# A norm listed earlier, a projection spread further and one more key buffer in a two-layer hybrid decoder

## The chip, the cores and the metric

One core of one Trainium2 chip runs the whole kernel in one launch. The metric is the device time of the core in microseconds, the median of several runs.

## The reference

Two decoder layers over 1024 positions of width 1024, all in float32. Cut to what matters:

```python
for layer in range(2):
    h = rms_norm(x, norm_mix[layer])
    q_a, k_a, v_a, q_h, f_h, i_h, g_h = split(h @ w_in[layer])
    attn = dilated_attention_group(q_a, k_a, v_a)       # 8 heads of 64; windows (128,1), (512,4), (2048,16)
    attn = rms_norm(attn, attn_out_gain[layer])         # over all 512 columns of the 8 heads
    rec = hgrn2_group(q_h, f_h, i_h, g_h)               # 4 heads of 128, gated linear recurrence
    x = x + concat([attn, rec]) @ w_out[layer]
    h = rms_norm(x, norm_mlp[layer])
    x = x + square(relu(h @ w_up[layer])) @ w_down[layer]
return rms_norm(x, norm_final)
```

The attention of each head is done over three dilated windows, whose results are merged by their softmax denominators. The attention norm needs all eight heads of a position, so it can't start on a half of the sequence before the last head has finished that half.

## The kernel before

All activations are kept transposed, as tiles of 128 columns by 512 positions, and the sequence has two halves of 512. Every float32 product is done as three products of a high and a low part (`split`, L321: ScalarE writes the high part, VectorE the low part). Such a tile is one "slot" of 2 KB per partition, and there are 71 slots that all stages share. Tiles that belong to a fixed kind have pools of their own; `COUNT` (L38) holds how many buffers each pool has.

**The order of the work.** The kernel first lists all its operations in a program order, and `Program.order` (L137) then makes the order of each engine's instructions from it. It is a list planner: whenever an engine is free in its model, it takes the operation with the lowest number in the list among those whose inputs are ready and whose buffers are free. An operation may be taken ahead of the list, as long as it is not more than 60 us of TensorE work beyond the oldest operation not yet started (36 us for loads and stores, which SyncE issues; `LOOKAHEAD`, L40). It may not take a buffer that the operations before it in the list will need. On the chip each engine then runs its instructions in that fixed order, so an instruction that waits holds up all that stand behind it on its engine. SyncE's queue issues all loads and stores.

`weave` (L46) sets the program order between two streams: it always advances the one with the smallest count of steps over weight. `weave((a, 24), (b, 13))` thus takes 24 steps of `a` to 13 of `b`, and when one stream is empty, the rest of the other follows.

**The stage around the change.** In each layer the steps come as follows.
- Two HGRN stages (the recurrence woven with the projections), the second with the attention's first projection.
- Attention heads 0 to 3, six units each, woven with the attention's second projection (L1198).
- Attention heads 4 to 7, six units each, woven with `out_part(1)` (L1200). That is the output projection of the HGRN half: for each half of the sequence one step that loads 8 tiles of HGRN results, then 8 steps of one block each. A block (`gemm4`) is 12 matmuls of 512 columns, a load of the residual tile and an addition.
- `norm_attn(0)` and `norm_attn(1)`, the attention norm of each half (L1189): squares, a sum over partitions by matmul, logarithm and exponential, then four scaled tiles, each split in two.
- `out_part(0, xs, (0,))`, the output projection of the attention half for positions 0 to 511, then for the second half, woven with the norm ahead of the MLP.

An attention unit (`attention`, L1128) is one head's 256 queries against their keys. Units 0 and 1 of a head serve the first half, 2 and 3 the second, 4 and 5 are the strided far window, which goes to the second half alone. A unit does the scores (L941, two matmuls for each block of 128 queries: high and low part of the keys), the maximum and mask on VectorE with a statistic (`ls`), the exponential on ScalarE, transposes, and the products with the values. After unit 1 of head 7 the last row of the first half is divided (`divide`, L991); after unit 5 the second half's is merged (`merge`, L998). Both send statistics through DRAM: a transpose on TensorE (`lt`), a copy (`lrow`), a store, a load, in `merge` small steps of VectorE and ScalarE (`ml`, `mw`) and another store, and a load that spreads the result over partitions (`rb`).

**The keys.** `Head.k` (L903) loads a head's high and low keys into two buffers of pool `kk`, 4 KB per partition each, by two DMAs each. Before, the pool has three. The MLP's up projection uses the same pool (`norm_up`, L1208): `hilo(..., "b11", p < COUNT["kk"])` puts an operand pair in a `kk` buffer for as many of its four pairs as there are buffers, and in two slots otherwise.

Of the kernel before, what the change touches and what calls it, by code (L numbers as in the profile page):

```python
# [34 lines left out]
EARLY = 10  # L35


COUNT = {"kk": 3, "slot": 71, "raw": 4, "trig": 2, "whi": 8, "wlo": 8, "ls": 4, "last": 2, "row": 2, "rc": 4, "z": 2, "gemm": 3, "sc": 2, "tr": 2, "acc": 1,  # L38
         "dram": 1 << 20, "const": 1 << 20}
LOOKAHEAD = {"PE": 60e3, "SP": 36e3}  # L40
PATIENCE = 5e3
# [4 lines left out]
def weave(*parts):  # L46

    live = [[0, *p] if isinstance(p, tuple) else [0, p, 1] for p in parts]
    while live:
        part = min(live, key=lambda p: p[0] / p[2])  # L50
        part[0] += 1
        if next(part[1], live) is live:
            live.remove(part)
# [69 lines left out]
class Program:  # L123
# [13 lines left out]
    def order(self):  # L137
        free = dict(COUNT)
        busy = {e: 0.0 for e in self.LATENCY}
# [30 lines left out]
        while done < len(self.ops):  # L170
            while oldest < len(self.ops) and self.ops[oldest].start is not None:
                oldest += 1
            for e in ready:
# [3 lines left out]
                while ready[e]:  # L177
# [12 lines left out]
                    for t, at in need.items():  # L190
                        h = held[t][oldest:max(at)]
                        ok = ok and free[t] >= len(at) and (not len(h) or h.max() + len(at) <= COUNT[t])
                    if not ok:
# [61 lines left out]
def trunk(ctx: ExitStack, tc: tile.TileContext, xT, wts, cols, trig, toep, lmask, ident_d, out):  # L255
# [7 lines left out]
    dram = ctx.enter_context(tc.tile_pool(name="dram", bufs=1, space=bass.MemoryType.DRAM))  # L263
    pools = {t: sbuf for t in COUNT}
    pools.update({t: psum for t in ("gemm", "sc", "tr", "acc")}, dram=dram, const=const)
# [25 lines left out]
    def slot(name, dt=F32, shape=None, width=None):  # L291
        return Buf(name, "slot", shape or [128, W], dt, width)

    def bank(name, tag, width=None):
        return Buf(name, tag, [128, W], F32, width)
# [13 lines left out]
    def tt(dst, a, b, kind, n=W, extra=()):  # L309

        op("DVE", c_tt(n), [dst[0]], [x[0] for x in (a, b) if x[0] is not None] + list(extra),
           lambda e: V.tensor_tensor(dst[1](), a[1](), b[1](), op=kind))  # L312

    def whole(b):
        return b, lambda: b.t
# [27 lines left out]
    def load(dst, view, src, nbytes, src_buf=None, join=False):  # L343
        op("SP", max(650.0, nbytes / 360.0), [dst], [src_buf] if src_buf else [], lambda e: nc.sync.dma_start(view(), src()), join=join)
# [46 lines left out]
    def gemm4(ps, grps, m, hf, acts, ts=slice(0, W)):  # L391
        gemm(ps, [grps[m // 4].piece(m % 4)], [x[hf] for x in acts], ts)
# [118 lines left out]
    def table():  # L511
        return [[None] * NH for _ in range(KT)]
# [4 lines left out]
    def load_x(src, k, hf):  # L517
        x = slot(f"x{k}_{hf}")
        i, j = rows(k, hf)
        saved = src and src[k][hf]  # L520
        if saved:
            load(x, lambda: x.t, lambda: saved.t, 1 << 18, saved)
        else:
            load(x, lambda: x.t, lambda: xT[i, j], 1 << 18)
        return x
# [16 lines left out]
    xs, hs, rs, xsaved = table(), table(), {}, None  # L542
# [34 lines left out]
    for l in range(L):  # L577
# [363 lines left out]
        def scores(hd, n, st, at):  # L941

            sp, t, ps = [], None, None
            k2 = [hd.k(part) for part in range(2)]
            for i, (q, q0, keys, x0) in enumerate(blocks(hd, n)):
                w = len(range(*keys.indices(S)))
                if t is None or o + w > W:
                    t, ps, o = slot("sp"), bank("sc", "sc"), 0

                def emit(e, ps=ps, q=q, q0=q0, keys=keys, o=o, w=w):  # L950
                    for part, k in enumerate(k2):
                        PE.matmul(ps[:, o:o + w], lhsT=q[:, q0:q0 + 128], rhs=k[:, keys], start=part == 0, stop=part == 1)  # L952

                op("PE", 2 * c_mm(w), [ps], [q] + k2, emit, join=o > 0)

                def emit(e, ps=ps, t=t, o=o, w=w, m=st.part(at + i), x0=x0):
                    V.tensor_tensor_reduce(t[:, o:o + w], ps[:, o:o + w], tpt[:, x0:x0 + w], -0.125, 3e38,  # L957
                                           OP.add, OP.min, m.t)

                op("DVE", c_tt(w), [t, st.part(at + i)], [ps, tpt], emit, join=True)  # L960
                sp.append((t, o, w))
                o += w
            return sp

        def soft(sp, st, at):
            for i, (t, o, w) in enumerate(sp):
                m, sum_ = st.part(at + i), st.part(at + 8 + i)
                op("ACT", c_act(w) + 190, [t, sum_], [t, m], lambda e, t=t, o=o, w=w, m=m, sum_=sum_: A.activation(  # L968
                    t[:, o:o + w], t[:, o:o + w], AF.Exp, bias=m.t, scale=-1.0, accum_out=sum_.t), "ln", True)
# [21 lines left out]
        def divide(st, ar):  # L991

            cs = slice(8, 16)
            op("DVE", 110.0, st.all(cs), st.all(cs), lambda e: V.reciprocal(st.buf[:, cs], st.buf[:, cs]))
            rb = spread(rows_of(st, cs), 0, "rb")
            tt(whole(ar), whole(ar), whole(rb), OP.mult)
# [131 lines left out]
        def attention(units):  # L1128
            for h, n in units:
                key = h  # L1130
                if key not in heads:
                    heads[key] = Head(h)
                hd, p, hf = heads[key], h // 2, int(n > 1)
                if (p, hf) not in stats:
                    stats[p, hf] = Stats()
                    left[p, hf] = 8 if hf else 4
                    araw[p][hf] = slot(f"ar{p}_{hf}")
                if n > 3 and p not in far_:
                    far_[p] = [slot("ar4") for _ in range(2 if p in SIDE else 1)]
                st = stats[p, hf]  # L1140
                at = 16 * (n > 3) + h % 2 * 4 + n % 2 * 2
                sp = scores(hd, n, st, at)
                soft(sp, st, at)
                if n > 3 and p in SIDE:
                    strided(h, n, sp, far_[p][n % 2])
                else:
                    values(h, n, sp, far_[p][0] if n > 3 else araw[p][hf])
                left[p, hf] -= 1
                if not left[p, hf]:
                    if hf:  # L1150
                        merge(st, araw[p][1], far_[p])
                    else:
                        divide(st, araw[p][0])
                yield
# [3 lines left out]
        def out_part(part, xs, hfs=(0, 1)):  # L1158
            acts, grp = mixed[4 * part:4 * part + 4], grp_out[part]
            for hf in hfs:  # L1160
                if part:
                    for h in range(HH):
                        pair = []
                        for d in hout[h][hf]:
                            y = slot("mh", F32R)
                            load(y, lambda y=y: y.t.bitcast(F32), lambda d=d: d.t, 1 << 18, d)
                            pair.append(y)
                        mixed[4 + h][hf] = pair
                    acts = mixed[4:]
                    yield  # L1170
                for m in range(KT):
                    if part:
                        xs[m][hf] = load_x(xsaved, m, hf)
                    ps = bank("pso", "gemm")
                    gemm4(ps, grp, m, hf, acts)
                    tt(whole(xs[m][hf]), whole(xs[m][hf]), whole(ps), OP.add)
                    yield
# [8 lines left out]
        def units(hs_, ns):  # L1186
            return [(h, n) for h in hs_ for n in ns]

        def norm_attn(hf):  # L1189
            r = rstd([araw[k][hf] for k in range(4)], 512, "an", hf == 0)  # L1190
            yield
            for k in range(4):
                t = slot("ant")
                stt(whole(t), whole(araw[k][hf]), lambda c=C_ATT + l * 4 + k: col(c), whole(r))
                mixed[k][hf] = hilo(t, f"ma{k}_{hf}")
                yield

        weave((attention(units(range(0, 4), range(6))), 26), (attn_proj(1), 12))  # L1198
        xs = table()
        weave((attention(units(range(4, 8), range(6))), 24), (out_part(1, xs), 13))  # L1200
        weave(norm_attn(0))
        weave(norm_attn(1))
        weave(out_part(0, xs, (0,)))

# [3 lines left out]
        def norm_up(hf):  # L1208
# [8 lines left out]
            for p in range(4):  # L1217
# [3 lines left out]
                if hf == 0:  # L1221
                    bo["11"].append(hilo(hf32[p][0], "b11", p < COUNT["kk"]))
                    bo["21"].append(hilo(hf32[p + 4][0], "b21"))
# [144 lines left out]
        xs = table()  # L1368
# [93 lines left out]
        last = l + 1 == L  # L1462
# [16 lines left out]
    for o in prog.order():  # L1479
        for b in o.fresh:  # L1480
            single = b.tag in ("dram", "const")
            b.tile = pools[b.tag].tile(b.shape, b.dt, name=b.name, tag=b.name if single else b.tag,
                                       bufs=1 if single else COUNT[b.tag])
        if o.on == "ACT" and o.table and o.table != loaded:
# [91 lines left out]
```

## Time and profile before

| | |
|---|---|
| median of 3 runs | 2428.82 us (2427.02 to 2429.88) |
| the profiled execution | 2435.95 us |
| its span, first to last instruction | 2434.2 us |
| TensorE busy | 2390.8 us (98%) |
| VectorE busy | 1733.8 us (71%) |
| ScalarE busy | 1217.5 us (50%) |
| DMA queue of SyncE | 404.93 MB, 49.7% of 16 engines' span |
| mean granted TensorE clock | 0.993 |

How to read it: PE is TensorE, DVE is VectorE, ACT is ScalarE, SPq is SyncE's queue. A row names an instruction by its line, what it writes and what it reads (`sc<-k,hd`: scores from keys and a head's queries). A bracket behind a row is the idle time before it and what ended it. The granted clock is a share of the full 2.4 GHz. In the first layer the two attention stages run from about 345 to 585 us, in the second from about 1550 to 1790.

### The profile page before, as it was taken

The page shows a single profiled execution, that of the slowest core. Times are in us where ns is not written, and L with a number is a line of the kernel's source. Part 1 is how long each engine was busy: PE and PEld are TensorE (multiplying, and loading weights), DVE is VectorE, ACT ScalarE, POOL GpSimd, SP SyncE. Part 2 cuts the span into 40 slices and gives each one's busy share as a digit, 9 for nine tenths or more (in the row PEclk, how much of TensorE's full clock was granted, in tenths as well). Part 3 has the DMA queues.
Part 4 walks back from the last instruction along what each step waited for, and adds up shares of the span by engine and source line. Part 5 has one row for each costly group of instructions (what it writes and reads, how often), then busy time and mean ns, then how long its engine had stood idle before and what let it go on. Part 6 is the DMA issues. An engine that isn't in the chain of part 4 may idle for free.

```text
span 2434.2 us, 35321 instructions
## 1 busy us (share of the span) xinstructions
PE 2390.8 (98%) x12572; PEld 2029.5 (83%) x12572; DVE 1733.8 (71%) x3414; ACT 1217.5 (50%) x2391; POOL 0.2 (0%) x4
## 2 busy tenths in 40 slices
PE   9999999999999999999999999999999999999998
PEld 7888898887888878888888988898878888888887
DVE  6365877778988667765744668677889885786575
ACT  7233346665744554445532433466656455554453
POOL 0000000000000000000000000000000000000000
PEclk9999999999999999999999999999999999999999
DMA  4011365953455469656420114668344653786562
GB/s 177 27 35 53 130 212 174 272 159 122 160 207 195 152 216 317 222 181 226 169 83 18 62 53 150 209 177 267 120 165 147 225 181 138 261 310 224 182 218 94
DMA packets 189681, 407.19 MB, mean 167 GB/s; under 512 B 22656, under 2 KB 25536, under 8 KB 189504
## 3 DMA queue, kind: packets, MB, share of 16 engines
q1 hardware_dynamic: 189504, 404.93, 49.7%
q8 instruction: 99, 1.62, 0.3%
q14 instruction: 78, 0.64, 0.1%
HBM read 291.37 MB, written 113.48 MB: 166 GB/s over the span
## 4 chain that ended last, share of the span: by engine, by line
PE 91%; DMA 4%; DVE 2%; ACT 2%; SPq 0%; issue 0%; DVEq 0%; ACTq 0%
PE psd L1415 8%; PE psd L1416 8%; PE psd L1417 8%; PE psu L1264 8%; PE psu L1265 8%; PE psu L1266 8%; PE sc L952 2%; PE pa L705 2%; PE pso L383 2%; PE pso L382 2%; PE pso L384 2%; PE pv L1115 1%; PE psv L407 1%; PE psq L382 1%; PE psv L408 1%; PE psv L409 1%
## 5 line engine op out<-in xcount | busy, mean ns | idle before, releaser
L325 DVE TENSOR_TENSOR al<-al,ah 128x512 fp32r<-128x512 f32 x224 | 152.7, 686 | 51.3 <-ACT ah L323 50.7
L323 ACT CAST ah<-al 128x512 fp32r<-128x512 f32 x224 | 137.4, 618 | 97.9 <-DMA al<-a 50.9
L968 ACT ACTIVATE sp<-sp,ls 128x256 f32<-128x256 f32 (+2 forms) x192 | 100.0, 523 | 17.7 <-DVE ls L957 17.3
L957 DVE CUSTOM_DVE_ANT_0 sp<-sc,tpt 128x256 f32<-128x256 f32 (+1 forms) x192 | 83.1, 439 | 35.6 <-PE sc L952 34.0
L952 PE MATMUL sc<-k,hd 128*128 128x256 f32 (+3 forms) x384 | 95.0, 358 | 12.7 <-DMA k<-kl 7.2
L952 PEld LDWEIGHTS sc<-k,hd 128*128 128x128 f32 x384 | 61.2, 195 | 19.6 <-DVE ls L957 6.1
L1247 ACT ACTIVATE c<-c 128x512 f32<-128x512 f32 x96 | 60.5, 630 | 33.2 <-DVE c L312 33.0
L323 ACT CAST pth<-ptr 128x512 fp32r<-128x512 f32 (+1 forms) x96 | 51.3, 552 | 39.5 <-PE ptr L1102 38.1
L1248 ACT ACTIVATE c<-c 128x512 f32<-128x512 f32 x108 | 68.4, 633 | 3.4
L325 DVE TENSOR_TENSOR ptl<-ptr,pth 128x512 fp32r<-128x512 f32 (+1 forms) x96 | 60.7, 641 | 10.9 <-ACT pth L323 9.8
L705 PEld LDWEIGHTS pa<-q,k 128*112 128x112 f32 (+3 forms) x512 | 62.0, 184 | 3.4
L705 PE MATMUL pa<-q,k 128*112 128x64 f32 (+3 forms) x512 | 61.2, 262 | 0.0
L312 DVE TENSOR_TENSOR x<-x,psd 128x512 f32<-128x512 f32 (+1 forms) x68 | 41.8, 652 | 25.3 <-PE psd L1417 25.1
L312 DVE TENSOR_TENSOR x<-x,pso 128x512 f32<-128x512 f32 x64 | 43.4, 681 | 15.2 <-PE pso L384 14.7
L1102 PE MATMUL ptr<-ident,sp 128*128 128x128 f32 x352 | 53.3, 276 | 0.5 <-ACT sp L968 0.4
L1264 PE MATMUL psu<-bt3h,s3h 128*128 128x512 f32 x128 | 50.6, 395 | 3.2 <-ACT u L319 3.2
L1122 ACT COPY pvt<-pv 64x256 f32<-64x256 f32 x80 | 29.6, 370 | 47.0 <-PE pv L1115 45.5
L713 DVE COPY_PREDICATED at<-lmt,pa 126x256 f32<-126x256 uint8 (+1 forms) x64 | 32.8, 512 | 25.1 <-PE pa L705 24.4
L1265 PE MATMUL psu<-bt3l,s3h 128*128 128x512 f32 x128 | 50.3, 393 | 0.0
L1266 PE MATMUL psu<-bt3h,s3l 128*128 128x512 f32 x128 | 50.3, 393 | 0.0
L1265 PE MATMUL psu<-bt1l,s1h 128*128 128x512 f32 x128 | 49.8, 389 | 0.0
L1266 PE MATMUL psu<-b22h,s4l 128*128 128x512 f32 x128 | 49.8, 389 | 0.0
(4980 smaller groups left out, 8136.0 us busy)
## 6 DMA issues: line engine op xcount, KB each, us to landing
al<-a SPq DMA_DIRECT2D x96, 256.0 KB
w0u<-in_wts_dram SPq DMA_DIRECT2D x42, 512.0 KB
w1u<-in_wts_dram SPq DMA_DIRECT2D x42, 512.0 KB
a<-c SPq DMA_DIRECT2D x76, 256.0 KB
al<-a0t SPq DMA_DIRECT2D x64, 256.0 KB
al<-a1t SPq DMA_DIRECT2D x64, 256.0 KB
hd<-q SPq DMA_DIRECT2D x48, 256.0 KB
a0t<-t SPq DMA_DIRECT2D x48, 256.0 KB
```

The costliest lines, as they stand in the source:

```text
L312: lambda e: V.tensor_tensor(dst[1](), a[1](), b[1](), op=kind))
L323: op("ACT", c_act(n), [hi[0]], [src[0]], lambda e: A.copy(hi[1](), src[1]()), join=join)
L325: lambda e: V.tensor_tensor(lo[1](), src[1](), hi[1]().bitcast(F32), op=OP.subtract), join=join)
L705: PE.matmul(pa[0:128 - b, c * 64:c * 64 + 64], lhsT=k[:, c * 128:c * 128 + 128 - b], rhs=by_half(q)[:, c, :, 1, :], start=True, stop=True)
L952: PE.matmul(ps[:, o:o + w], lhsT=q[:, q0:q0 + 128], rhs=k[:, keys], start=part == 0, stop=part == 1)
L968: op("ACT", c_act(w) + 190, [t, sum_], [t, m], lambda e, t=t, o=o, w=w, m=m, sum_=sum_: A.activation(t[:, o:o + w], t[:, o:o + w], AF.Exp, ...
L1264: PE.matmul(ps.t, lhsT=wh[:, cs], rhs=xh.t, start=first and k == 0, stop=False, skip_group_check=True)
L1265: PE.matmul(ps.t, lhsT=wh[:, cs], rhs=xl.t, start=False, stop=False, skip_group_check=True)
L1266: PE.matmul(ps.t, lhsT=wl[:, cs], rhs=xh.t, start=False, stop=k == 3, skip_group_check=True)
L1415: PE.matmul(ps.t, lhsT=wh[:, cs], rhs=th.t[:, ts], start=first and j == 0, stop=False, skip_group_check=True)
L1416: PE.matmul(ps.t, lhsT=wh[:, cs], rhs=tl.t[:, ts], start=False, stop=False, skip_group_check=True)
L1417: PE.matmul(ps.t, lhsT=wl[:, cs], rhs=th.t[:, ts], start=False, stop=j == 15, skip_group_check=True)
```

## The change

There are three edits. The key pool gets a fourth buffer, and the slots go from 71 to 69, which is the same memory. By the expression in `norm_up` all four pairs then lie in key buffers. The first half's norm is put into the attention's stream of steps between unit 2 and unit 3 of head 7; it has five steps, so the stream has 29. The weights of that weave go from 24 : 13 to 34 : 13.

```diff
-COUNT = {"kk": 3, "slot": 71, "raw": 4, "trig": 2, "whi": 8, "wlo": 8, "ls": 4, "last": 2, "row": 2, "rc": 4, "z": 2, "gemm": 3, "sc": 2, "tr": 2, "acc": 1,
+COUNT = {"kk": 4, "slot": 69, "raw": 4, "trig": 2, "whi": 8, "wlo": 8, "ls": 4, "last": 2, "row": 2, "rc": 4, "z": 2, "gemm": 3, "sc": 2, "tr": 2, "acc": 1,
...
         weave((attention(units(range(0, 4), range(6))), 26), (attn_proj(1), 12))
         xs = table()
-        weave((attention(units(range(4, 8), range(6))), 24), (out_part(1, xs), 13))
-        weave(norm_attn(0))
+        last = itertools.chain(attention(units(range(4, 7), range(6)) + units((7,), range(3))), norm_attn(0),
+                               attention(units((7,), range(3, 6))))
+        weave((last, 34), (out_part(1, xs), 13))
         weave(norm_attn(1))
         weave(out_part(0, xs, (0,)))
```

## Rows read from the trace of the kernel before

**Rows 1.** the page, part 1: busy us, share, instructions
```profile
PE 2390.8 (98%) x12572; PEld 2029.5 (83%) x12572; DVE 1733.8 (71%) x3414; ACT 1217.5 (50%) x2391; POOL 0.2 (0%) x4
```

**Rows 2.** windows: us, busy by engine (count), clock, DMA share, GB/s
```profile
340.00:585.00 245.00, 231.90 (x1376) 201.77 (x1375) 190.35 (x477) 150.36 (x397) 0.00 (x0) 0.99 0.61 183
585.00:890.00 305.00, 305.00 (x1340) 251.35 (x1340) 239.93 (x384) 172.91 (x295) 0.00 (x0) 1.00 0.51 178
1545.00:1790.00 245.00, 233.21 (x1367) 202.67 (x1366) 189.49 (x476) 149.26 (x396) 0.00 (x0) 0.97 0.59 182
```

**Rows 3.** TensorE's waits, first layer's attention: total, times, longest
```profile
PE sc L952 <- DMA k<-kl: 4.0, 4, 1.9
...
PE pso L382 <- ACT ma_0h L323: 1.5, 1, 1.5
...
PE pso L383 <- DVE ma_0l L325: 0.7, 1, 0.7
```

**Rows 4.** the same view, second layer's attention
```profile
PE sc L952 <- DMA k<-kl: 3.2, 3, 2.2
PE sc L952 <- DVE ls L957: 3.0, 2, 2.5
...
PE pso L383 <- DVE ma_0l L325: 0.4, 1, 0.4
```

**Rows 5.** windows of 5 us behind gaps, both layers
```profile
495.00:500.00 5.00, 3.11 (x15) 2.56 (x13) 2.53 (x7) 2.05 (x4) 0.00 (x0) 0.84 1.05 276
500.00:505.00 5.00, 5.00 (x31) 4.69 (x30) 2.41 (x8) 2.59 (x10) 0.00 (x0) 0.82 0.76 216
555.00:560.00 5.00, 4.19 (x11) 2.88 (x11) 4.77 (x10) 1.94 (x4) 0.00 (x0) 0.66 0.00 0
1580.00:1585.00 5.00, 5.00 (x21) 4.12 (x20) 2.82 (x11) 2.92 (x10) 0.00 (x0) 0.66 1.03 265
1755.00:1760.00 5.00, 2.08 (x11) 1.34 (x10) 4.89 (x10) 3.55 (x7) 0.00 (x0) 0.79 0.04 8
1760.00:1765.00 5.00, 5.00 (x13) 3.79 (x14) 4.41 (x10) 1.65 (x3) 0.00 (x0) 0.53 0.00 0
```

**Rows 6.** timeline, SyncE's queue, first layer: start, us, instruction
```profile
354.85 0.35 SPq L344 DMA_DIRECT2D hd<-q  x1
368.16 1.12 SPq L344 DMA_DIRECT2D k<-kl  x2
```

**Rows 7.** windows of heads 4 to 7, line L382's instructions alone
```profile
452.00:474.50 22.50, 4.98 (x12) 2.27 (x12) 1.00 0.87 237
474.50:495.00 20.50, 5.66 (x14) 2.67 (x14) 1.00 0.93 292
495.00:521.00 26.00, 6.50 (x16) 3.06 (x16) 0.93 0.53 146
521.00:553.00 32.00, 8.91 (x22) 4.18 (x22) 1.00 0.39 125
```

**Rows 8.** timeline of VectorE, end of the first layer's attention
```profile
544.18 0.69 DVE L312 TENSOR_TENSOR ar<-ar,rb 128x512 f32<-128x512 f32 x1
...
553.13 0.74 DVE L455 SCALAR_TENSOR_TENSOR ant<-ar,colt,anrs 128x512 f32<-128x512 f32 x1
...
558.91 0.37 DVE L312 TENSOR_TENSOR mw<-ml 8x128 f32<-8x128 f32 x1
```

**Rows 9.** timeline of TensorE, the same place and behind it
```profile
550.19 0.27 PE L975 MATMUL lt<-ident,ls 128*32 128x128 f32 x1
...
554.58 0.49 PE L382 MATMUL pso<-ma_0h,w0o000h 128*128 128x512 f32 x1 [1.53 <-ACT ma_0h L323]
...
568.45 0.39 PE L382 MATMUL pso<-ma_0h,w0o010h 128*128 128x512 f32 x1
...
580.23 0.39 PE L382 MATMUL pso<-ma_1h,w0o000h 128*128 128x512 f32 x1
```

## The prediction

> **What bounds the kernel now.** First the busy shares: TensorE is busy for 2390.8 of 2434.2 us [rows 1], so every gain has to come from its 43 us of idle time, from stretches in which its clock is halved, or from other work getting out of its way. Then the stretches by stage: the attention of each layer (340 to 585 and 1545 to 1790) holds 13.1 and 11.8 us of that idle time, while the 305 us after the first has none [rows 2]. The change touches just this stage in both layers. Then what TensorE waited for there. In the first layer the score matmuls stand 4.0 us for keys that a DMA brings, and the output projection 1.5 and 0.7 us for the two parts of the normed attention output [rows 3]. In the second layer these are 3.2 us for keys and 0.4 us for the low part of the normed output, and 3.0 us behind the statistics that VectorE reads out with the scores [rows 4]; the row for the high part is the same there, word for word.
>
> Last the clock. It falls to its lower level of 1.2 GHz behind some of these gaps. In a 5 us window with a mean clock of 0.84 the lost time is 5 x 0.16 = 0.8 us. Behind the key gap at 497 the windows show 0.84 and 0.82, together 1.7 us; behind the key gap of 2.2 us at 1578 they show 0.66, 1.7 us; behind the first half's norm they show 0.66 at 555 (1.7 us) and 0.79 with 0.53 at 1755 (3.4 us) [rows 5]. The same pair of gaps cost twice as much in the second layer as in the first.
>
> Run against profile: the profiled execution took 2435.95 us, the median of the runs is 2428.82, 7.1 us (0.3%) less. The terms below are microseconds out of the profile and are taken off the median unscaled.
>
> **The change part by part.**
>
> *Fourth key buffer (T1).* A head needs two key buffers, its high and its low part. With three, the next head's low part can be loaded only when the last score matmul of the current head has let one go. SyncE takes its list in order: after the query load at 354.85 nothing is issued until the low keys go out at 368.16, 13 us in which every later load and store stands behind that one instruction [rows 6]. With four, both parts of the next head have free buffers as soon as the head before the current one is done, a head (20 to 32 us, [rows 7]) ahead. No instruction is added and no byte more moves. At most this takes away 4.0 + 3.2 = 7.2 us of gaps [rows 3, 4] and 1.7 + 1.7 = 3.4 us of slow clock [rows 5], 10.6 us. At least it gives nothing, if another load comes late in the keys' place: the DMA engines are 0.87 and 0.93 busy in heads 4 and 5 [rows 7]. But the keys of heads 1 to 3 are loaded before that, and with them go 2.1 of the first layer's 4.0 us (all but the longest, 1.9, which is head 6's) and the second layer's 2.2 us wait, so I stay near the upper end: **-8 us**.
>
> *First half's norm listed before the last three units (T2).* The norm's instructions (squares and their sum, two sum matmuls, logarithm and exponential, four scaled tiles and their split) are the same in number and hold no DMA; only their rank in the planner's list changes. In the trace the first half's row is divided at 544.18, the first scaled tile comes at 553.13 [rows 8], and the projection starts on it at 554.58 after its 1.53 us wait [rows 9]. Had the tiles been there, TensorE would have lost neither 1.5 + 0.7 + 1.7 us in the first layer nor 1.5 + 0.4 + 3.4 in the second (the 0.4 is its wait for the low part) [rows 3 to 5], 9.2 us together. But the second half's work sets a later end: from the transpose of the last statistics at 550.19 to the first product with the second half's tile at 580.23 are 30.0 us, a chain of DMAs to DRAM and back, small VectorE steps and another norm [rows 9]. The only work under it is the first half's projection: four blocks of it run from 568.45 to 580.23 [rows 9], less about 0.9 us for the sum matmuls in between, so 2.7 us a block and 22 us for its eight. If that starts earlier and the chain doesn't, the time comes back as a wait at the head of the second half. The chain can start earlier, since VectorE does the norm's eight tile operations right before the merge's first step at 558.91, with 5.4 us of norm work between 553.13 and there (5.8 us less one 0.4 us addition) [rows 8]. Bounds 0 and -9.2; I take half, **-4.6 us**.
>
> *What the norm displaces (T3).* Ranked higher, its 5.4 us of VectorE work per layer stands ahead of the last three units' score and value steps, in order. TensorE has blocks of the projection to run meanwhile, so I count **0**. If that cover is gone, the merge chain starts up to 5.4 us later in each layer, +10.8 us. The gain on the other side, a chain that starts earlier, is in T2.
>
> *HGRN projection spread (T4).* Before, the 18 steps of this projection go 13 to 24 attention steps; now 13 to 34, over 29 steps with the norm's five. When the last unit is listed, 11 rather than 13 steps are, so 7 rather than 5 are left behind it: 2 blocks, 5.4 us more work that can lie under the merge chain. Against that, the loads are listed later, and SyncE looks only 36 us of TensorE work ahead. Four products of the first weight form make a block, so heads 4 to 7 used 3, 3.5, 4 and 5.5 blocks as filler [rows 7], more than any list order demands: the filler is taken whenever attention has to wait. In head 6 (six units, 34 / 13 = 2.6 to a step) the new list lets loads go out for about 6 / 2.6 = 2.3 steps, of which one loads the second half's HGRN tiles: 1.3 new blocks and what is left over, against 4 used. If 1.6 blocks lack there, 1.6 x 2.7 = 4.4 us a layer stand idle; if attention runs through faster for it, nothing; if the lighter load traffic ends the second layer's wait for the statistics, 3.0 us are won [rows 4]. I take the end nearer to the filler rows but small, **+2 us** for both layers, since the work not done there lies under the chain later.
>
> *Two general buffers fewer (T5).* In the up projection nothing changes: its fourth pair of operands moves from two general buffers into the fourth key buffer, so 71 - 2 and 69 leave the same 69. Elsewhere 3% fewer buffers mean less prefetch. Where TensorE has no gap [rows 2] the cover holds; in attention the loads may come later. Between 0 and 7.2 us (as much as the keys cost, [rows 3, 4]); **+1.5 us**.
>
> Sum: -8 - 4.6 + 0 + 2 + 1.5 = -9.1 us; 2428.8 - 9.1 = 2419.7, forecast **2420 us**.
>
> Two rules are weighed beside this. On the clock: the Trainium skill (TensorE: Matmul & The Clock Gate, "What's actually happening") says that the slow clock is the default which activity lifts, and that the monitor behind it runs free of the kernel's start. By it a gap need not cost its drop, nor does a drop go for certain with its gap; the sum without clock terms would have T1 at 7.2 and T2 at 4.1 at most. The unequal price of the same two gaps [rows 5] agrees. On transfers: the Trainium skill (DMA: Bandwidth & Descriptors, "Specifications") gives some 358 GB/s of HBM to a core. By that the 237 and 292 GB/s of heads 4 and 5 [rows 7] leave room to load keys earlier and all of T1 could come; by their busy shares there is hardly any.
>
> **The rivals.**
> - *Everything goes.* Key gaps, norm gaps and their drops all vanish, because the spread leaves enough filler for the chain: -10.6 - 9.2 = -19.8, **2409 us**. For it: 5.4 us of extra filler against the 30 - 22 = 8 us that the chain now outlasts its projection blocks. Against it: DMA shares near full [rows 7].
> - *The norm's gain is handed back.* The chain doesn't move, T2 is zero, and of the keys only the waits outside heads 5 and 6 go: 4.0 - 1.9 (the longest, at head 6) = 2.1, and 3.2, and one drop of 1.7, 7.0; less T4 and T5, -3.5: **2425 us**. For it: the chain's DMAs are untouched. Against it: 5.4 us of VectorE work leaves the chain's start.
> - *Slower: the merge chain starts late.* The norm ahead of the last units holds VectorE for 5.4 us, so the last scores, the statistics' transpose and all behind it slip; TensorE runs out of filler and its clock falls, 5.4 + 1.7 a layer, 14.2 in all, less 8 for the keys: +6.2, **2435 us**. It decides from the point at which filler left behind the last unit is under 30 + 5.4 us; 22 of first-half projection plus two to five blocks of 2.7 is 27 to 36, so it is close. Against it: the divided row is ready only at 544.18 [rows 8], when the last scores are nearly done.
> - *The change doesn't do what it says.* The general buffers run short, the query and value loads keep SyncE as late as before, and the keys come no sooner: no change, **2429 us**. For it: 3% fewer buffers in a stage that fills them; against it: the low keys are freed by their own pool alone.
>
> **How the numbers follow.** Chances: forecast 0.42 (own range 2413 to 2424), everything 0.18, handed back 0.21, slower 0.15, nothing done 0.04. A measurement of this kernel can tell about 0.2%, 4.9 us, from no change. Faster by more than that (under 2424): the first two and a little of the third, 0.63. Within it: 0.22, the rest of the third and the fifth. Slower: 0.15. The range for 8 in 10 reaches from below the second case to between the third and the fourth: 2406 to 2433.
>
> **What would show it.** T1: no wait of the score matmuls for keys in the list of waits, both key loads issued about a head ahead, no 13 us hole in SyncE's list. T2: the norm's scaled tiles done before the last value products, no wait at the first projection product, and the time from the statistics' transpose to the second half's first product under 30 us, or covered. T3 and T4: the transpose no later against the end of head 6, and HGRN blocks still running under the chain. T5: no new waits for queries, values or weights, and TensorE still without gaps outside attention. The forecast is wrong if the idle time of the two attention stages (25 us now) falls by less than 4 us, if it reappears as waits of the second half's projection, or if other stages grow.

## The result, and the profile after

The changed kernel takes 2414.03 us (2408.34 to 2417.86, 7 runs) against 2427.02 us before (2420.86 to 2429.88, 7 runs, the three of the table above among them). The ratio is 0.9938, with a 95% interval of 0.9927 to 0.9949: 15.0 us of 2427 (12.4 to 17.7). The two medians lie 13.0 us apart, which the interval holds; below, all times go by the ratios. The forecast was 2420 us, with 2406 to 2433 as its range.

The two profiled executions lie further apart: 2435.95 and 2411.42 us. The one of before is 8.9 us above its median of seven, the one of after 2.6 below, so by the medians 11.5 of the 24.5 us between them belong to these two executions and not to the change. The views below show where time went; its amount is taken from the runs.

Page and stages of the changed kernel (windows: us, busy of TensorE, its loads, VectorE, ScalarE, GpSimd, clock, DMA share, GB/s):

```profile
span 2409.6 us, 35371 instructions
...
PE 2380.3 (99%) x12572; PEld 2025.0 (84%) x12572; DVE 1730.1 (72%) x3414; ACT 1215.3 (50%) x2391; POOL 0.2 (0%) x4
```

```profile
340.00:585.00 245.00, 239.51 (x1413) 209.91 (x1413) 197.39 (x491) 157.46 (x409) 0.00 (x0) 0.99 0.63 195
585.00:890.00 305.00, 305.00 (x1341) 251.28 (x1340) 240.46 (x386) 172.86 (x297) 0.00 (x0) 1.00 0.52 179
1545.00:1790.00 245.00, 238.82 (x1413) 208.84 (x1412) 199.48 (x491) 158.72 (x411) 0.00 (x0) 0.99 0.60 188
```

The idle time of TensorE went from 13.1 and 11.8 us in the two attention stages to 5.5 and 6.2, and the stage behind is as full as it was [rows 2]. What TensorE still waits for in the whole kernel (total, times, longest):

```profile
PE ptr L1102 <- ACT sp L968: 3.1, 6, 0.7
PE pv L1115 <- DVE ar L1124: 2.2, 5, 0.6
PE sc L952 <- DVE ls L957: 2.2, 2, 1.1
...
PE pv L1115 <- DVE ptl L325: 1.6, 3, 1.0
...
PE pso L382 <- ACT w1o110h L323: 1.4, 1, 1.4
...
PE sc L952 <- DMA hd<-q: 1.0, 2, 0.8
```

No score matmul waits for keys, and no projection matmul for a normed tile, in either layer [rows 3, 4]. What is left in the two attention stages stands behind exponentials, the rows that value products add to, low parts of transposed exponentials, statistics, queries and, once in the second layer, a weight cast.

SyncE's queue at the place of [rows 6] (start, us, instruction):

```profile
343.32 1.09 SPq L344 DMA_DIRECT2D k<-kh  x2
344.45 1.24 SPq L344 DMA_DIRECT2D k<-kl  x2
...
354.51 0.58 SPq L344 DMA_DIRECT2D hd<-q  x1
367.09 0.48 SPq L344 DMA_DIRECT2D k<-kh  x1
```

Both parts of the keys of head 1 go out at 343 and 344; before, the low part left at 368.16. But the queue still stands from 354.51 to 367.09, now for the keys of head 2: the fourth buffer has moved what waits there one head on, and not ended the hole.

The clock at its two drops in these stages, and a window at the place where the first half's norm cost one before [rows 5]:

```profile
465.00:470.00 5.00, 4.19 (x16) 3.89 (x17) 2.71 (x9) 2.01 (x6) 0.00 (x0) 0.58 0.54 186
470.00:475.00 5.00, 5.00 (x22) 3.97 (x21) 4.42 (x10) 3.70 (x10) 0.00 (x0) 0.74 1.00 268
...
545.00:550.00 5.00, 5.00 (x24) 4.13 (x23) 4.48 (x11) 3.14 (x7) 0.00 (x0) 1.00 0.01 2
...
1670.00:1675.00 5.00, 3.65 (x17) 2.83 (x16) 2.61 (x9) 2.10 (x7) 0.00 (x0) 0.91 0.93 329
1675.00:1680.00 5.00, 5.00 (x27) 4.36 (x26) 4.04 (x13) 4.22 (x14) 0.00 (x0) 0.74 0.82 193
```

The lost time is 5 x (0.42 + 0.26) = 3.4 us in the first layer and 5 x (0.09 + 0.26) = 1.8 us in the second; before it was 3.4 and 6.8 (the 6.8 with a pair of windows at 1660 that [rows 5] leave out). At 545 the clock is full.

The end of the first layer's attention on VectorE, then on TensorE:

```profile
527.31 0.69 DVE L312 TENSOR_TENSOR ar<-ar,rb 128x512 f32<-128x512 f32 x1 [1.55 <-DMA rb<-l]
...
535.20 2.08 DVE L455 SCALAR_TENSOR_TENSOR ant<-ar,colt,anrs 128x512 f32<-128x512 f32 x3 [1.36 <-ACT anrs L319]
...
544.38 0.37 DVE L312 TENSOR_TENSOR mw<-ml 8x128 f32<-8x128 f32 x1
```

```profile
534.91 0.27 PE L975 MATMUL lt<-ident,ls 128*32 128x128 f32 x1
534.94 0.48 PE L382 MATMUL pso<-mh,w0o103h 128*128 128x512 f32 x1
...
547.27 0.39 PE L382 MATMUL pso<-mh,w0o113h 128*128 128x512 f32 x1
...
547.95 0.39 PE L382 MATMUL pso<-ma_0h,w0o000h 128*128 128x512 f32 x1
...
569.39 0.40 PE L382 MATMUL pso<-ma_1h,w0o000h 128*128 128x512 f32 x1
```

The cast of the second half's first normed tile on ScalarE, before and then after:

```profile
578.48 1.94 ACT L323 CAST ma_1h<-ant 128x512 fp32r<-128x512 f32 x3 [0.82 <-DVE ant L455]
```

```profile
563.42 1.95 ACT L323 CAST ma_1h<-ant 128x512 fp32r<-128x512 f32 x3 [0.82 <-DVE ant L455]
```

The last row of the first half is divided at 527.31, the first scaled tile starts at 535.20, 9.2 us ahead of the merge's first step at 544.38, and it is used only at 547.95, behind the last HGRN block. From the transpose of the last statistics at 534.91 to the second half's first product at 569.39 are 34.5 us [rows 9: 30.0]. They are filled by four HGRN blocks, seven and a half of the eight of the first half and the last value products, with two gaps of 0.3 us before 542. The chain itself is as long as it was: the first tile's cast starts 28.3 us behind the transpose before and 28.5 after. What grew is the work under it; the tile is used 6.0 us after its cast starts, before it was 1.8. The HGRN blocks in the stretches of heads 4 to 7, the last up to 541, can be counted from line L382, four instructions to a block:

```profile
447.00:465.00 18.00, 3.31 (x8) 1.55 (x8) 1.00 0.83 233
465.00:495.00 30.00, 6.84 (x16) 3.31 (x16) 0.89 0.90 265
495.00:514.00 19.00, 3.96 (x10) 1.92 (x10) 1.00 0.63 207
514.00:541.00 27.00, 8.90 (x22) 4.17 (x22) 1.00 0.25 77
```

That is 2, 4, 2.5 and 5.5 blocks, and the other 2 behind 541, against 3, 3.5, 4 and 5.5 with none left [rows 7].

### The profile page after: what moved, and what is told of

It reads as the page before. It is cut to its first block, busy times and chain, and to the rows that moved or that the text cites. A ratio compares the mean times of both kernels' runs of the same rounds, so it can differ in the third digit from the quotient of the medians.

```text
span 2409.6 us, 35371 instructions
## 1 busy us (share of the span) xinstructions
PE 2380.3 (99%) x12572; PEld 2025.0 (84%) x12572; DVE 1730.1 (72%) x3414; ACT 1215.3 (50%) x2391; POOL 0.2 (0%) x4
## 4 chain that ended last, share of the span: by engine, by line
PE 93%; DMA 2%; DVE 2%; ACT 1%; SPq 0%; issue 0%; DVEq 0%
PE psd L1416 8%; PE psd L1418 8%; PE psd L1417 8%; PE psu L1265 8%; PE psu L1266 8%; PE psu L1267 8%; PE sc L952 2%; PE pa L705 2%; PE pso L382 2%; PE pso L384 2%; PE pso L383 2%; PE pv L1115 2%; PE psva L407 1%; PE psv L407 1%; PE psb L382 1%; PE psq L382 1%
## 5 line engine op out<-in xcount | busy, mean ns | idle before, releaser
L968 ACT ACTIVATE sp<-sp,ls 128x256 f32<-128x256 f32 (+2 forms) x192 | 99.9, 523 | 10.2 <-DVE ls L957 10.0
L312 DVE TENSOR_TENSOR x<-x,psd 128x512 f32<-128x512 f32 (+1 forms) x68 | 41.8, 652 | 24.9 <-PE psd L1418 24.9
L312 DVE TENSOR_TENSOR x<-x,pso 128x512 f32<-128x512 f32 x64 | 43.1, 682 | 14.1 <-PE pso L384 12.5
L312 DVE TENSOR_TENSOR u<-u,psu 128x512 f32<-128x512 f32 x40 | 27.4, 684 | 33.9 <-PE psu L1267 33.9
L1122 ACT COPY pvt<-pv 64x256 f32<-64x256 f32 x80 | 29.5, 369 | 42.9 <-PE pv L1115 39.5
L713 DVE COPY_PREDICATED at<-lmt,pa 126x256 f32<-126x256 uint8 (+1 forms) x64 | 32.8, 512 | 25.1 <-PE pa L705 24.5
```

## The experiments

My theory was additive: the keys bring about 8 us, the norm and the spread the rest. Rival K gave everything to the keys, rival N everything to the new list. The three edits (K: keys and slots, N: norm, S: spread) were run alone and in all pairs; together with the two kernels that makes all eight combinations. Ratios are against the kernel before on the same chip; times in us are the ratio's distance from 1 times 2427.

**K alone.**

```diff
-COUNT = {"kk": 3, "slot": 71,
+COUNT = {"kk": 4, "slot": 69,
```

> The kernel before with the fourth key buffer and 69 slots, the order of the work listed as before. Additive theory (keys, norm and spread each bring a part): 7 to 9 us faster, the score matmuls' 7.2 us of waits for keys gone, the wait for the first half's normed tiles (1.5 + 0.7 us in layer one) still there. Rival K (the keys bring everything, also by freeing SyncE's queue): 13 to 15 us faster. Rival N (the new list brings everything): within 3 us of before.

Measured 2418.88 us, ratio 0.9958 (0.9945 to 0.997): 10.2 us faster. Two waits of TensorE in its first layer:

```profile
PE ptr L1102 <- ACT sp L968: 4.0, 3, 2.8
PE pso L382 <- ACT ma_0h L323: 2.5, 1, 2.5
```

The waits for keys are gone, the one for normed tiles is longer than in [rows 3]. The time lies between the additive theory and rival K, nearer to the first.

**N and S without K.**

```diff
+        last = itertools.chain(attention(units(range(4, 7), range(6)) + units((7,), range(3))), norm_attn(0),
+                               attention(units((7,), range(3, 6))))
+        weave((last, 34), (out_part(1, xs), 13))
```

> The new list (norm before the last three units, weights 34 to 13) with three key buffers and 71 slots. Additive theory: 5 to 7 us faster, the wait for the normed tiles gone, the last statistics transposed some 10 us earlier against the end of the projection, the waits for keys still 5 to 8 us. Rival K: within 3 us of before. Rival N: 13 to 15 us faster.

Measured 2429.67 us, ratio 1.001 (0.9999 to 1.0021): no gain, where the additive theory had 5 to 7 us. Its first layer:

```profile
PE pso L382 <- ACT ma_1h L323: 3.4, 1, 3.4
...
PE sc L952 <- DMA k<-kl: 1.8, 2, 1.4
```

The wait for the first half's tile is gone, and one of 3.4 us for the second half's stands in its place. The statistics are transposed 5.9 us earlier than before, not some 10. So the norm's gain is handed back here, and neither the additive theory nor rival N holds.

**N alone.**

```diff
-        weave((last, 34), (out_part(1, xs), 13))
+        weave((last, 24), (out_part(1, xs), 13))
```

(against the experiment before)

> Only the norm moved before the last three units, weights left at 24 to 13, three key buffers. If the merge chain sets the end (the prediction's reason for taking half): 0 to 3 us faster, the gap moves from the first half's projection to the head of the second half's. If the normed tiles alone were late: 7 to 9 us faster. If the norm's VectorE work delays the chain: up to 14 us slower.

Measured 2435.32 us, ratio 1.003 (1.0019 to 1.004): 7.3 us slower, which only the third expectation allows. Its first layer:

```profile
PE pso L382 <- ACT ma_1h L323: 3.4, 1, 3.4
PE sc L952 <- DMA k<-kl: 3.1, 2, 2.0
...
PE pso L383 <- DVE ma_0l L325: 0.5, 1, 0.5
...
PE pso L382 <- ACT ma_0h L323: 0.3, 1, 0.3
```

The same wait for the second half's tile, and 0.8 us for the first half's are left. The last scores start at 545.98 us rather than 539.73, but the statistics are transposed only 1.4 us later. TensorE's idle time in the two attention stages is 26.1 us against 24.9 before; what grew is the time lost to the clock, 18.9 us against 10.2 (5 us windows, one execution each). In the first layer much of it is lost at the two projections:

```profile
555.00:560.00 5.00, 4.59 (x11) 3.63 (x12) 4.96 (x9) 2.17 (x4) 0.00 (x0) 0.50 0.31 102
...
585.00:590.00 5.00, 4.75 (x11) 3.83 (x12) 3.35 (x6) 0.86 (x2) 0.00 (x0) 0.50 0.40 152
```

With their neighbours these windows lose 3.4 us each; before, it was 1.7 us at the first place and nothing at the second. The move by itself makes two gaps out of one, and in this execution both cost a drop.

**S alone.**

```diff
-        weave((attention(units(range(4, 8), range(6))), 24), (out_part(1, xs), 13))
+        weave((attention(units(range(4, 8), range(6))), 34), (out_part(1, xs), 13))
```

> Only the weights of the weave changed to 34 to 13, the norm listed behind as before, three key buffers. If filler is rationed by the later loads (the prediction's T4): 0 to 4 us slower. If the spread by itself lets the attention run through earlier and leaves blocks for the merge chain: 3 to 6 us faster, with the last statistics transposed 5 us or more earlier against the end of the projection.

Measured 2431.17 us, ratio 1.0011 (1.0001 to 1.0021): 2.7 us slower, inside the first expectation. Its first layer:

```profile
PE pso L382 <- ACT ma_0h L323: 2.9, 1, 2.9
...
PE pso L383 <- DVE ma_0l L325: 1.1, 1, 1.1
```

The statistics are transposed at 545.39 rather than 550.19, 4.8 us earlier and so nearly as the second expectation had it, but the first half's tiles now come later against the work, 2.9 + 1.1 us instead of 1.5 + 0.7. The profiled execution (2425.84 us) is one of the fastest of its twelve, so it doesn't show where the 2.7 us lie.

**K and N.** The first experiment's edit and the third's.

> Fourth key buffer, 69 slots and the norm before the last three units, weights left at 24 to 13. Chain theory (with the keys early the last units finish sooner; the norm's gain is kept only if enough projection blocks lie under the merge chain): the wait for the first half's tiles is gone, a wait of 1 to 3 us for the second half's tiles stands in its place in each layer, total 8 to 12 us faster than before, so 3 to 7 us behind the changed kernel. Rival (the keys alone make the norm's move pay, the spread is needless): 14 to 16 us faster, no wait for the second half's tiles.

Measured 2425.28 us, ratio 0.9989 (0.998 to 0.9998): 2.7 us faster, so 7.5 us of the keys' gain are lost, more than expected. Its first layer:

```profile
PE ptr L1102 <- ACT sp L968: 3.4, 2, 2.7
PE anms L439 <- DVE ansq L312: 2.0, 1, 2.0
...
PE pso L382 <- ACT ma_1h L323: 1.3, 1, 1.3
```

The second half is late again, now already at its sum of squares (2.0 us) and then at its tiles.

**K and S.** The first experiment's edit and the fourth's.

> Fourth key buffer, 69 slots and weights of 34 to 13, the norm listed behind as before. Chain theory: the wait of about 2.5 us for the first half's tiles stays in each layer with its drop of the clock, 8 to 11 us faster than before. Rival (the spread is what the keys alone lacked): 13 to 16 us faster.

Measured 2424.69 us, ratio 0.9984 (0.9975 to 0.9993): 3.9 us faster, 6.3 us behind K alone, and so below both expectations. Its first layer:

```profile
PE pso L382 <- ACT ma_0h L323: 2.9, 1, 2.9
PE pso L382 <- ACT w0o110h L323: 2.5, 1, 2.5
```

Beside the late first half there is a wait of 2.5 us for a projection weight (2.9 us in the second layer): ScalarE's cast of that weight, on its own timeline, had stood idle for 4.1 us until the load landed:

```profile
481.76 0.62 ACT L323 CAST w0o110h<-w0o 128x512 fp32r<-128x512 f32 x1 [4.11 <-DMA w0o<-in_wts_dram]
```

That load is issued at 472.61, with the keys alone at 470.97, and in both its cast starts some 9 us later, while the attention runs ahead (its last scores start at 525.90 instead of 532.89). That fits loads which the spread lists later and which then come too late; it was not shown by itself.

**Two slots fewer alone.**

```diff
-COUNT = {"kk": 3, "slot": 71,
+COUNT = {"kk": 3, "slot": 69,
```

> The kernel before with three key buffers and 69 slots: it leaves two slots (4 KB per partition) unused and prices them alone; the up projection's fourth operand pair still takes two slots, so that stage has 67. If slots are slack: within 2 us of before. If the stage is short of them (the prediction's T5): 1.5 to 7 us slower, by later loads in the attention or by gaps in the up projection.

Measured 2428.8 us, ratio 1.0004 (0.9996 to 1.0013): 1.0 us, not told apart from nothing. Slots are slack to that point.

What the eight combinations say, for the first layer (from the profiled executions: when the last statistics are transposed; how many HGRN blocks are still run behind that; how long behind it the cast of the second half's first tile starts, and the first product with it; and which normed tile TensorE waits for):

| kernel | us against before | transposed at | HGRN blocks behind | cast | product | waits for |
|---|---|---|---|---|---|---|
| before | 0 | 550.19 | 0 | 28.3 | 30.0 | first half, 1.5 |
| N | +7.3 | 551.62 | 0 | 31.7 | 32.4 | second half, 3.4; first half, 0.3 |
| S | +2.7 | 545.39 | 1.5 | 30.6 | 34.4 | first half, 2.9 |
| N, S | +2.4 | 544.34 | 1 | 29.6 | 30.3 | second half, 3.4 |
| K | -10.2 | 537.31 | 3.5 | 31.3 | 40.7 | first half, 2.5 |
| K, N | -2.7 | 547.29 | 0 | 28.0 | 28.6 | second half, 1.3 behind 2.0 |
| K, S | -3.9 | 530.71 | 4.5 | 30.7 | 42.7 | first half, 2.9 |
| K, N, S | -15.0 | 534.91 | 4 | 28.5 | 34.5 | neither |

Every kernel with the old place of the norm waits for the first half's tiles. In all eight the second half's first tile is cast 28 to 32 us behind the transpose, so the chain's length differs little. What differs is the work that TensorE has for that time: the first half's projection, 22 us, and what is left of the HGRN projection. The three kernels with the norm moved that wait for the second half have one HGRN block left or none, their work has run out when the tile comes, and it is used 0.7 us after its cast starts. The changed kernel has four blocks left, and no wait.

Keys and spread each pull the transpose forward (13 and 5 us, 19 together), the norm in its new place pushes it back when the keys are there (10 us from K, 4 from K and S) and hardly without them. These are single executions: with nothing changed but two slots fewer the transpose is at 547.84, so differences of 2 or 3 us say little. So the third edit pays only on top of the other two: with the keys, norm and spread cost 7.5 and 6.3 us each alone and bring 4.8 together. The 4.8 rest on two intervals that just meet (7.3 to 13.3 us for K, 12.4 to 17.7 for all three); the two variants of the changed kernel below that measure as it does, 14.6 and 13.3 us faster than before, bear them out.

**More spread.**

```diff
-        weave((last, 34), (out_part(1, xs), 13))
+        weave((last, 44), (out_part(1, xs), 13))
```

> The changed kernel with weights 44 to 13 instead of 34 to 13, so one more block or two is listed behind the last unit. If blocks under the merge chain are what pays: equal to the changed kernel or up to 3 us faster (13 to 18 us faster than before). If filler inside the attention is what is short now: 2 to 6 us behind the changed kernel, with new waits of TensorE in heads 5 to 7.

Measured 2413.69 us, ratio 0.994 (0.9928 to 0.9952): as the changed kernel. Under the chain lie five HGRN blocks instead of four, and neither more blocks there nor fewer before it matter at this point, where the tile was already waiting for TensorE.

**A longer allowance for transfers.**

```diff
-    LATENCY = {"PE": 210.0, "ACT": 190.0, "DVE": 190.0, "SP": 1800.0}
+    LATENCY = {"PE": 210.0, "ACT": 190.0, "DVE": 190.0, "SP": 3600.0}
```

> The changed kernel with the planner's allowance for a transfer's landing raised from 1.8 to 3.6 us, so that it plans nothing on a load as early as before. If what is left of the gaps (5.5 and 6.0 us a layer) comes from transfers that land later than planned (weights, queries): 3 to 8 us faster than the changed kernel, 16 to 23 faster than before. If the longer allowance only makes the planner put less work between: 0 to 10 us behind the changed kernel.

Measured 2448.06 us, ratio 1.0084 (1.007 to 1.0098): 20.4 us slower, worse than either expectation. Its waits:

```profile
PE anms L439 <- DVE ansq L312: 8.7, 2, 4.3
...
PE pso L382 <- ACT ma_1h L323: 5.5, 2, 2.7
```

The sum of squares of the second half alone is waited for 8.7 us, twice 4.3. With the longer allowance the statistics are transposed at 548.83, and the second half's first product comes at 589.03, 40 us behind and 0.7 us after the tile's cast starts; here the chain itself was stretched, from 28.5 to 39.5 us.

**A longer look ahead for loads.**

```diff
-LOOKAHEAD = {"PE": 60e3, "SP": 36e3}
+LOOKAHEAD = {"PE": 60e3, "SP": 48e3}
```

> The changed kernel with SyncE allowed to look 48 instead of 36 us of TensorE work ahead. If the loads of the spread projection come late because of that limit (T4): the wait of 1.35 us for projection weights in layer two and the 1.09 us behind late weights go, 2 to 5 us faster than the changed kernel. If the DMA engines or the slots are the limit: within 3 us of it.

Measured 2424.32 us, ratio 0.9985 (0.9976 to 0.9994): 11 us behind the changed kernel, outside both expectations. Its waits:

```profile
PE pv L1115 <- DVE ar L1124: 5.3, 6, 1.8
PE sc L952 <- DMA hd<-q: 3.4, 2, 2.4
```

The weight cast is no longer waited for, but queries are for 3.4 us instead of 1.0, and the value products for the rows they add to. That fits loads that go earlier crowding out those needed next; it was not shown by itself.

**The norm behind the fourth unit.**

```diff
-units((7,), range(3))), norm_attn(0), attention(units((7,), range(3, 6))))
+units((7,), range(4))), norm_attn(0), attention(units((7,), range(4, 6))))
```

> The changed kernel with the norm listed behind the fourth instead of the third unit of the last head. If the norm only has to be done before the merge chain's end: within 2 us of the changed kernel. If its place decides which work lies under the chain: 3 to 6 us behind, with a wait for the first half's tiles.

Measured 2414.67 us, ratio 0.9945 (0.9932 to 0.9959): as the changed kernel. Behind the third or the fourth unit is the same; other places were not run.

**A shorter look ahead for loads.**

```diff
-LOOKAHEAD = {"PE": 60e3, "SP": 36e3}
+LOOKAHEAD = {"PE": 60e3, "SP": 28e3}
```

> The changed kernel with SyncE's look ahead cut from 36 to 28 us of TensorE work. 48 us made it some 11 us slower. If early loads crowd out the ones that are needed next (queries, weights): 2 to 5 us faster than the changed kernel, the wait for queries gone. If 36 us is where the planner's order happens to fall well: 3 to 12 us behind the changed kernel, with new waits for loads.

Measured 2439.59 us, ratio 1.0047 (1.0033 to 1.0061): 11.4 us slower than before, some 26 behind the changed kernel, twice what the second expectation allowed. The wait for queries is not gone either (1.6 us against 1.0), and the longest waits are those of value products, 4.7 us for the rows that they add to and 3.8 for low parts of transposed exponentials. So the first expectation fails, and the reading that early loads crowd out others at 48 us gets no support from it. 36 us lies between two worse values, and no version that was run beats the changed kernel beyond the intervals.

## Why the prediction was right, and where not

- *T1, the keys.* Forecast -8, with +1.5 for the slots (T5), -6.5 together. K alone holds both and measured -10.2 (7.3 to 13.3 us faster), which is near the 10.6 us that T1 named as its most; the slots alone +1.0, not told apart from nothing. The waits for keys are gone as forecast. The sign named for it was half wrong: the loads go out a head ahead, but the hole in SyncE's queue stayed, since the keys of the head after next stand in it. That it did no harm is seen, that it could not is not shown.
- *T2, the norm.* Half of 9.2 us was taken on the ground that the second half's chain sets the end. The ground was right: N without the other edits turns the wait for the first half into one of 3.4 us for the second in each layer. The hope in it was not: the chain does not start earlier with the norm's VectorE work out of its way, the merge's first step comes 8.7 us behind the transpose before (550.19 to 558.91) and 9.5 us after (534.91 to 544.38). The size was not a property of this step. Alone it is +7.3 us, and +7.5 on top of the keys; only with keys and spread is the wait gone on both sides, and there the norm brings 11.1 us (3.9 to 15.0), more than the bound of 9.2.
- *T3, what the norm displaces.* Counted 0, with +10.8 at most. This is the term that was mis-sized where the cover is missing: N alone is 7.3 us slower. That it is slower is what the rival "the merge chain starts late" says, but not by its road: the last scores start 6.2 us later in the first layer, the transpose only 1.4 us, and in the profiled execution the loss lies in the clock (8.7 us more lost than before) and hardly in idle time (1.2 us more). On top of the keys the transpose slips by 10 us, more than the 5.4 us of VectorE work that the rival named; why was not followed.
- *T4, the spread.* Forecast +2; alone it measured +2.7. Of the 2 blocks more that it was to leave under the chain, S alone leaves 1.5, and on top of K and N it leaves 4. Filler was not what lacked but weights: on top of the keys it costs 6.3 us, with a wait for a projection weight, which the second layer of the changed kernel still has (1.4 us).
- *The sum.* T2 to T4 were added as -2.6 us and measured -4.8 on top of the keys, but as an interaction: N and S, each measured alone on top of the keys, would add up to +13.8. The total fell between the forecast and "everything goes" (2409 us), whose reason, enough blocks under the chain, is what the trace of the changed kernel shows. The sum came out near by terms that were wrong in both directions: that the forecast holds is in part luck.
- *The clock.* Of the 8.5 us of drops named by T1 and T2 all four places are clear in the profile after, but a new drop of 3.4 us stands behind the waits at 462 to 466, and one of 1.8 us at 1675. In the kernel before, gaps of 1.3 us at 374 and 1.0 us at 527 have no drop behind them. The Trainium skill (TensorE: Matmul & The Clock Gate, "What's actually happening") says that "the default state is throttled, and activity releases the throttle". That a gap need not cost a drop, which the prediction took from this, agrees with those two gaps. That a drop need not shrink with its gap is seen in N alone: at the first half's projection of the first layer the waits shrink from 2.2 to 0.8 us and the loss grows from 1.7 to 3.4 us, in one execution of each kernel.
- *Left open.* Which part of the keys' gain comes from the missing waits and which from other heads' work being planned closer together was not separated. Why 28 and 48 us of look ahead both cost more than 10 us was followed only as far as the waits named above. Where the 2.7 us of S alone lie is open too.

## What to carry to other kernels

A step moved ahead of a critical chain has two sides: what it saves at its own place, and what it takes from the work that covers the chain; measure from the chain's start to its use and ask what is left to lie under it. Edits that each lose alone can win together, so run the pairs before an edit is thrown out or praised. In a kernel whose order a planner makes, a constant that looks like a safety margin (a latency, a look ahead) moves everything: here doubling the one cost 35 us, and the other lay between two worse values.

## What was not expected of the hardware

Executions of one and the same kernel differ by 9.5 us here (2408.34 to 2417.86) and by 12.5 us for S alone (2424.26 to 2436.74), more than any term of the sum. In the 5 us windows of both profiles the time lost to the clock comes in pieces of about 1.7 us or twice that, and the length of a gap doesn't tell which: in the changed kernel three gaps of 0.5 to 0.8 us between 462 and 466 went ahead of a loss of 3.4 us, and in N alone five gaps of 0.2 to 0.5 us between 551 and 556 did too, while in the kernel before single gaps of 1.3 us at 374 and 1.0 us at 527 had none behind them.
